# Up-projections of a two-layer trunk: all chunks 4 to 19 as pairs by seven products

## The chip, the cores and the metric

The kernel runs on one core of a Trainium2 chip. The metric is the device time of one execution in microseconds (us), the median of several runs. Five engines of the core work side by side, each through its own list of instructions in order: TensorE (PE, with its weight load PEld), VectorE (DVE), ScalarE (ACT), GpSimd (POOL) and SyncE (SP), which issues most of the transfers. An instruction that needs the result of another engine waits for it, and everything behind it on its own engine waits as well.

## What is computed

The reference is a decoder trunk of two layers over 512 tokens with 1024 channels in float32. A layer is an attention part and a feed-forward part, each with its norms and residual sums. The change concerns the first matrix product of the feed-forward part, whose inner size D_FF is 2816:

```python
def conv_ffn(xn, w_up, cw, cb, w_down):
    a = xn @ w_up                       # (512 x 1024) @ (1024 x 5632)
    ap = jnp.pad(a, ((0, 0), (CONV_W - 1, 0), (0, 0)))
    a = sum(ap[:, j:j + T] * cw[j] for j in range(CONV_W)) + cb
    gate, val = jnp.split(a, 2, axis=-1)
    return (jax.nn.gelu(gate, approximate=True) * val) @ w_down
```

## The kernel before

**Precision.** A float32 product is made of three passes of PE: each operand is split into a high part (a cast to `float32r`) and a low part (the operand less its high part), and `mm3` (L291) adds high x high (L292), high x low (L293) and low x high (L294). So each weight piece needs a cast on ACT and then its low half. The low half comes either from a DVE subtract, or in two steps: ACT writes the negated piece, rounded like the high part, to the place of the low part (a minus), and a transfer that POOL issues adds the unrounded piece to it in SBUF (an accumulating transfer, `accum_op=ALU.add`).

**Chunks.** The 2816 gate columns and 2816 value columns are taken in 22 chunks of 128 columns. A chunk has a gate half and a value half, each a PSUM bank of 128 columns by 512 tokens. A plain chunk loads two weight pieces of 1024 channels by 128 columns and does 8 channel blocks x 3 passes for each half, 48 matmuls over 512 tokens (`up`, L956).

**Seven products.** In the chunks listed in `SEVEN` (L28), 11 of the chunks 4 to 19, the product is written as a 2 x 2 block product: the weights in blocks by gate or value and by half of the channels (a11 and a12 for the gate, a21 and a22 for the value), the activations by half of the channels and half of the tokens (`LO`, `HI`). Seven products of sums replace eight: A11, S2, S3, A12, S1, A22 and S4, named by the weight block or sum of blocks in each, every one 4 channel blocks x 3 passes over 256 tokens (`half_mm`, L952), 84 matmuls in all. The sums of activations (`XA`, `XB`) are made once a layer (`sums_in`, L686). The sums of weights are made for each chunk by DVE (`weights_a`, L720, `weights_b`, L754). The sums of results are made on DVE in PSUM and in small tiles called `csum`, of which the first is an ACT copy of A11's result (L1000). In the program's order, the weights of a chunk are prepared one or two chunks ahead by generators whose steps the main loop (L978) advances between the products.

**Behind the product.** For each chunk, ACT writes the conv's last tap and bias to a tile `bb` (L655), DVE adds the two shifted taps for each half with two instructions (L656, L658), ACT applies GELU (L676), DVE multiplies gate and value (`product`, L673) and a transfer stores the result for the second matrix product (L671).

The instructions of each engine stand in the order in which the code emits them. Waits are derived from the tiles that an instruction reads and writes; a copy of one half of a PSUM bank and a product into the other half of it count as the same tile. The tiles come from rotating pools: `p8` (16 of 4 KB), `p4` (10) and `p2` (8), and 8 PSUM banks.

Of the kernel before, what the change touches and what calls it, by code (L numbers as in the profile page):

```python
# [27 lines left out]
SEVEN = 4, 5, 7, 8, 10, 11, 13, 14, 16, 17, 19  # L28

ADDED = (6, 9, 12, 15, 18), (18, 20)  # L30
# [87 lines left out]
def trunk_kernel(ctx, tc, x, norm_gains, w_qkv_a, w_o_a, w_q_b, w_o_b, kv_norm, w_kvf, b_f,  # L118
# [62 lines left out]
    def add_ffn(l):  # L181
        for c in range(NF):
            add_cols(w_up[l], c * 128)
            add_cols(w_up[l], DFF + c * 128)
# [461 lines left out]
    def ffn(l, bd, cp, nxt, ahead):  # L646
# [3 lines left out]

        def taps(c, banks, between=None):
            bb = t4([128, 2, T], name="bb")
            for s, ch in ((0, c), (1, NF + c)):
                ps = banks[s]
                act.activation(bb[:, s, :], ps, AF.Identity, bias=cp[:, 3, ch:ch + 1], scale=cp[:, 2, ch:ch + 1])  # L655
                dve.scalar_tensor_tensor(bb[:, s, 1:], ps[:, :T - 1], cp[:, 1, ch:ch + 1], bb[:, s, 1:],  # L656
                                         ALU.mult, ALU.add)
                dve.scalar_tensor_tensor(bb[:, s, 2:], ps[:, :T - 2], cp[:, 0, ch:ch + 1], bb[:, s, 2:],  # L658
                                         ALU.mult, ALU.add)
                if s == 0 and between is not None:  # L660
                    between()
            return bb
# [3 lines left out]
        def product():  # L666

            if gated:
# [4 lines left out]
                dve.tensor_tensor(hc[c], bb[:, 0, :], bb[:, 1, :], ALU.mult)  # L673
# [31 lines left out]
        halves, rest, late = {}, {}, []  # L705

        def split_pair(pair, src, n=1024):
            act.copy(pair[:, 0, :n], src)
            yield
            dve.tensor_tensor(pair[:, 1, :n], src, pair[:, 0, :n].bitcast(F32), ALU.subtract)  # L710

        def add_low(w, raw):

            act.activation(w[:, 1], raw, AF.Copy, scale=-1.0)
            pool.dma_start(w[:, 1], raw, accum_op=ALU.add)

        def sub_low(w, raw, n=1024):
            dve.tensor_tensor(w[:, 1, :n], raw, w[:, 0, :n].bitcast(F32), ALU.subtract)

        def weights_a(c):  # L720


            if c >= NF:
                return
            if c not in SEVEN:
                for i in range(2):
                    if c in ADDED[i]:
                        W.high_added()
                    else:
                        W.high()  # L730
                        W.low()
                    yield
                return
            r0, r1 = W.take(2)
            w = [t8([128, 2, 1024], F32R, name="w") for _ in range(2)]
            sa, sb = (t4([128, 1024], name="wsum") for _ in range(2))
            a11, a12, a21, a22 = r0[:, 0:512], r0[:, 512:1024], r1[:, 0:512], r1[:, 512:1024]
            act.copy(w[0][:, 0], r0)
            if c - 1 not in SEVEN:
                add_low(w[0], r0)  # L740
            dve.tensor_tensor(sa[:, 0:512], a11, a21, ALU.subtract)
            dve.tensor_tensor(sb[:, 0:512], a21, a22, ALU.add)
            yield
            dve.tensor_tensor(sa[:, 512:1024], sb[:, 0:512], a11, ALU.subtract)
            if c - 1 not in SEVEN:
                act.copy(w[1][:, 0], sa)
                add_low(w[1], sa)
            v = [t.rearrange("p s (q k c) -> p s q k c", q=2, k=4) for t in w]
            halves[c] = dict(A11=v[0][:, :, 0], A12=v[0][:, :, 1], S3=v[1][:, :, 0], S2=v[1][:, :, 1])
            rest[c] = w, r0, a12, a22, sa, sb  # L750

        def weights_b(c):

            if c not in rest:  # L754
                return
            (w0, w1), r0, a12, a22, sa, sb = rest.pop(c)
            if c - 1 in SEVEN:
                act.copy(w1[:, 0], sa)
                sub_low(w0, r0)
            w = [t8([128, 2, 1024], F32R, name="w") for _ in range(2)]  # L760
            dve.tensor_tensor(sb[:, 512:1024], a12, sa[:, 512:1024], ALU.subtract)
            act.copy(w[1][:, 0, 0:512], a22)
            if c - 1 in SEVEN:
                sub_low(w1, sa)
            yield
            act.copy(w[0][:, 0], sb)
            if c - 1 in SEVEN:
                late.append(lambda: sub_low(w[0], sb))
            elif c < SEVEN[-1]:
                add_low(w[0], sb)  # L770
            sub_low(w[1], a22, 512)
            if c == SEVEN[-1]:
                sub_low(w[0], sb)
            v = [t.rearrange("p s (q k c) -> p s q k c", q=2, k=4) for t in w]
            halves[c].update(S1=v[0][:, :, 0], S4=v[0][:, :, 1], A22=v[1][:, :, 0])
            yield

# [197 lines left out]
        steps = iter(())  # L975
        begun = None
        before = None
        for c in range(2, NF):  # L978
            if c == NF - 4:
                pair_load(0)  # L980
            steps = chain(steps, weights_b(c + 1), weights_a(c + 2))
            if c + 2 == SEVEN[0]:
                steps = chain(steps, weights_b(c + 2))
            if c in SEVEN:
                w = halves.pop(c)
                W.n_get += 2
                x11, x21, x22 = [(xT[0][i], xT[1][i], s) for i, s in ((0, LO), (1, LO), (1, HI))]
                if begun:
                    banks, s1, s17 = begun
                else:  # L990
                    banks = [bank([128, T], name="up") for _ in range(2)]
                    s1, s17 = (t2([128, 256], name="csum") for _ in range(2))
                s12 = t2([128, 256], name="csum")
                o1, o2, o3, o4 = banks[0][:, LO], banks[0][:, HI], banks[1][:, LO], banks[1][:, HI]

                def prod(o, a, x, start=False, w=w):
                    half_mm(o, w[a], x[0:2], x[2], start)

                def begin():
                    act.copy(s1, o1)  # L1000
                    prod(o3, "S3", (*XA, HI), True)
                    dve.tensor_tensor(s17, o3, s1, ALU.add)
                    prod(o2, "S2", (*XB, HI))

                def join():
                    dve.tensor_tensor(s12, o2, s1, ALU.add)

                if begun:
                    prod(o2, "S2", (*XB, HI))
                    product()  # L1010
# [899 lines left out]
```

## Time and profile before

| | us |
|---|---|
| time of one execution, median of 3 | 1096.97 (1096.6 to 1098.53) |
| span of the profiled execution | 1095.3 |
| PE busy in it | 1088.0 |
| DVE busy | 882.3 |
| ACT busy | 667.5 |
| POOL busy | 154.4 |

The profile is one execution. A row of a timeline has the start in us from the span's begin, the duration, the engine, the line of the code, the operation, what is written and read, and the shape; in brackets stands how long the engine had been idle and what released it. Neighbouring instructions of one kind can stand in one row with a count (x2). Durations of neighbours overlap by some 0.1 us, so the time an instruction occupies is read from the starts. A row of the grouped lines has the count, the total busy time, the mean duration in ns, and the idle time ahead with its releasers. A row of a window has its length, the busy time of PE, PEld, DVE, ACT and POOL with counts, the clock granted to PE as a share of full, the share of the transfer engines, and GB/s.

### The profile page before, as it was taken

What the parts mean: (1) busy time and instruction counts of PE and PEld (TensorE: products, weight loads), DVE (VectorE), ACT (ScalarE), POOL (GpSimd) and SP (SyncE); (2) the same over time, 40 slices, a digit from 0 to 9 for tenths busy, and PEclk for the clock granted to TensorE, in tenths of its full rate; (3) what the DMA queues carried; (4) which work ended last, traced back from release to release, by engine and by line L of the source; (5) the groups of instructions that cost most, each with busy time, mean ns of one, the idle gap of its engine ahead of it and who ended that gap; (6) DMA issues with size and microseconds to landing.
All of it is one profiled execution on the core that took longest, in us unless ns stands there. A gap on an engine that the chain in (4) does not pass through costs nothing.

```text
span 1095.3 us, 17965 instructions
## 1 busy us (share of the span) xinstructions
PE 1088.0 (99%) x6537; PEld 946.4 (86%) x6537; DVE 882.3 (81%) x1510; ACT 667.5 (61%) x1117; POOL 154.4 (14%) x240
## 2 busy tenths in 40 slices
PE   9999999999999999999999999999999999999997
PEld 7888889899999988888878888889899999988886
DVE  5898979877878789897686667858878788779895
ACT  6745665656666656576451587755755656647473
POOL 2643000111111111000001212100111111211000
PEclk9999999999999999999999999999999999999999
DMA  9899944668898979793447867784568978979872
GB/s 292 241 366 405 351 125 135 135 164 198 190 210 190 226 266 325 268 341 99 146 143 240 274 174 207 243 238 136 105 174 190 213 184 184 245 244 318 313 250 77
DMA packets 191984, 241.60 MB, mean 221 GB/s; under 512 B 12832, under 2 KB 139160, under 8 KB 191896
## 3 DMA queue, kind: packets, MB, share of 16 engines
q1 hardware_dynamic: 176552, 189.33, 53.6%
q0 software_dynamic: 14656, 51.13, 20.3%
q8 instruction: 51, 0.84, 0.3%
q14 instruction: 37, 0.30, 0.1%
q10 hardware_dynamic: 688, 0.01, 0.1%
HBM read 172.37 MB, written 39.73 MB: 194 GB/s over the span
## 4 chain that ended last, share of the span: by engine, by line
PE 95%; DMA 2%; issue 1%; DVE 1%; ACT 0%; SPq 0%; DVEq 0%; ACTq 0%; POOL 0%; POOLq 0%
PE up L294 12%; PE up L292 12%; PE up L293 12%; PE acc L292 9%; PE acc L294 9%; PE acc L293 9%; PE v_ps L293 2%; PE v_ps L292 2%; PE v_ps L294 2%; PE pT_ps L1751 2%; PE o_ps L1766 2%; PE s_ps L1717 2%; PE qk_ps L292 1%; PE first L292 1%; PE first L293 1%; PE first L294 1%
## 5 line engine op out<-in xcount | busy, mean ns | idle before, releaser
L292 PE MATMUL acc<-w 128*128 128x512 f32 (+1 forms) x311 | 120.5, 388 | 0.0
L294 PE MATMUL acc<-w 128*128 128x512 f32 (+1 forms) x311 | 120.4, 387 | 0.0
L293 PE MATMUL acc<-w 128*128 128x512 f32 (+1 forms) x267 | 103.2, 387 | 0.0
L292 PE MATMUL up<-xsh,w 128*128 128x256 f32 x352 | 99.6, 283 | 0.0
L293 PE MATMUL up<-xsl,w 128*128 128x256 f32 x352 | 99.6, 283 | 0.0
L294 PE MATMUL up<-xsh,w 128*128 128x256 f32 x352 | 99.6, 283 | 0.0
L655 ACT ACTIVATE bb<-up,conv 128x512 f32<-128x512 f32 x80 | 59.7, 776 | 59.2 <-DVE up L1046 48.4
L60 ACT CAST w<-wraw 128x1024 fp32r<-128x1024 f32 x81 | 83.2, 1051 | 18.6 <-DMA wraw<-in_w_up_dram 7.8
L294 PE MATMUL up<-xch,w 128*128 128x512 f32 (+1 forms) x276 | 93.5, 339 | 0.1
L292 PE MATMUL up<-xbh,w 128*128 128x512 f32 (+1 forms) x276 | 93.6, 339 | 0.0
L293 PE MATMUL up<-xcl,w 128*128 128x512 f32 (+1 forms) x276 | 93.5, 339 | 0.0
L293 PE MATMUL up<-xbl,w 128*128 128x512 f32 (+1 forms) x276 | 93.5, 339 | 0.0
L292 PE MATMUL up<-xch,w 128*128 128x512 f32 (+1 forms) x276 | 93.5, 339 | 0.0
L294 PE MATMUL up<-xbh,w 128*128 128x512 f32 (+1 forms) x276 | 93.4, 338 | 0.0
L78 DVE TENSOR_TENSOR w<-wraw,w 128x1024 fp32r<-128x1024 f32 x62 | 74.6, 1223 | 16.6 <-ACT w L60 16.2
L292 PEld LDWEIGHTS acc<-w 128*128 128x128 f32 x311 | 58.4, 188 | 11.9
L294 PEld LDWEIGHTS acc<-w 128*128 128x128 f32 x311 | 58.4, 188 | 11.8
L292 PEld LDWEIGHTS up<-xsh,w 128*128 128x128 f32 x352 | 67.6, 192 | 0.0
L293 PEld LDWEIGHTS up<-xsl,w 128*128 128x128 f32 x352 | 67.6, 192 | 0.0
L294 PEld LDWEIGHTS up<-xsh,w 128*128 128x128 f32 x352 | 67.6, 192 | 0.0
L656 DVE SCALAR_TENSOR_TENSOR bb<-up,conv,bb 128x511 f32<-128x511 f32 x80 | 59.5, 744 | 7.9 <-ACT bb L655 7.8
L98 POOL DMA_DIRECT2D w<-wraw x20 | 17.5, 876 | 336.8 <-ACT w L71 307.3
(317 smaller groups left out, 3112.8 us busy)
## 6 DMA issues: line engine op xcount, KB each, us to landing
wraw<-in_w_up_dram SPq DMA_DIRECT2D x88, 512.0 KB
w<-wraw POOLq DMA_DIRECT2D x32, 512.0 KB, 6.2
dT<-dsums SPq DMA_DIRECT2D x28, 512.0 KB
dsums<-in_w_down_dram SPq DMA_DIRECT2D x22, 512.0 KB
dsums<-in_w_down_dram SPq DMA_DIRECT2D x44, 256.0 KB
w<-wsum POOLq DMA_DIRECT2D x22, 512.0 KB, 5.6
hD<-hc POOLq DMA_DIRECT2D x44, 256.0 KB, 7.2
dact<-hD SPq DMA_DIRECT2D x44, 256.0 KB
```

The lines of the kernel that those rows point to most:

```text
L60: (copy or self.nc.scalar.copy)(pair[:, 0], raw)
L78: self.nc.vector.tensor_tensor(pair[:, 1], raw, pair[:, 0].bitcast(F32), ALU.subtract)
L98: self.nc.gpsimd.dma_start(pair[:, 1], raw, accum_op=ALU.add)
L292: pe.matmul(o, ah, bh, start=first, stop=False, skip_group_check=shared)
L293: pe.matmul(o, ah, bl, start=False, stop=False, skip_group_check=shared)
L294: pe.matmul(o, al, bh, start=False, stop=last, skip_group_check=shared)
L655: act.activation(bb[:, s, :], ps, AF.Identity, bias=cp[:, 3, ch:ch + 1], scale=cp[:, 2, ch:ch + 1])
L656: dve.scalar_tensor_tensor(bb[:, s, 1:], ps[:, :T - 1], cp[:, 1, ch:ch + 1], bb[:, s, 1:], ALU.mult, ALU.add)
L1717: pe.matmul(sc[j, i][hh][:, :nn], qT[j][own, qp, i * 128:(i + 1) * 128], k[own, kp, :nn], start=qp + kp == 0, stop=qp == 1)
L1751: pe.transpose(o[:, k0 + k, :], p[:, hh, k * 128:(k + 1) * 128], ident)
L1766: pe.matmul(o[64 * hh:64 * hh + 64, i * 128:(i + 1) * 128], Vt[hd // 8][:, k, (hd % 8) * 64:(hd % 8) * 64 + 64], pT[j, i, hh][:, k, :], st ...
```

## The change

`SEVEN` is replaced by `PAIRS`, pairs 2 to 9, so that chunks 4 to 19 all go by seven products, two chunks at a time. Chunks 2 and 3 ahead of them and 20 and 21 behind them stay plain.

- **Weight pieces.** A pair loads four pieces of half the channels by 256 columns: `ga` and `gb` of the gate, `va` and `vb` of the value. Each of the seven weight tiles of a pair is 1024 elements a partition and serves both chunks.
- **`prepare(p)`** (L728) makes the seven weight tiles in eight steps. `high` (L734) is a cast on ACT, `low` (L738) a subtract on DVE or POOL, and `added` (L741, L742) is the minus on ACT and the accumulating transfer. A12's low half and the sum `gb - ga` (L770) are on POOL; `ga - va` (L752), `va + vb` (L756) and `va - ga` (L758) on DVE. The low halves of S1, A22 and S4 come by accumulating transfers.
- **The gating product** (L686) is a POOL instruction.
- **Order of a pair on PE:** S2, S3, A12, S1, A22, then A11 of the next pair, then S4, each for both chunks. The steps of the next pair's preparation and the conv steps of the last pair's two chunks stand between them. All eight steps of the first pair's preparation stand in chunks 2 and 3, ahead of that pair's A11.
- **`keep_first`** (L1022) is the ACT copy of A11's results.

The core of the diff:

```diff
-SEVEN = 4, 5, 7, 8, 10, 11, 13, 14, 16, 17, 19
+PAIRS = range(2, 10)
...
+                for c0, k0 in ((0, 0), (DFF, 0), (DFF, 4), (0, 4)):
+                    add(lambda raw, c=c0 + c * 128, k0=k0: [(raw.rearrange("p (k c) -> p k c", k=4),
+                                                             cols(w_up[l], k0, 4, c, 256))])
...
-                dve.tensor_tensor(hc[c], bb[:, 0, :], bb[:, 1, :], ALU.mult)
+                pool.tensor_tensor(hc[c], bb[:, 0, :], bb[:, 1, :], ALU.mult)
...
+        def prepare(p):
+            def high(a, raw):
+                w[a] = t8([128, 2, 1024], F32R, name="w")
+                act.copy(w[a][:, 0], raw)
+                W2[p, a] = w[a].rearrange("p s (k c) -> p s k c", k=4)
+            def low(a, raw, engine=dve):
+                engine.tensor_tensor(w[a][:, 1], raw, w[a][:, 0].bitcast(F32), ALU.subtract)
+            def added(a, raw):
+                act.activation(w[a][:, 1], raw, AF.Copy, scale=-1.0)
+                pool.dma_start(w[a][:, 1], raw, accum_op=ALU.add)
+            w = {}
+            ga = grab(2)
+            high("A11", ga)
+            yield
+            low("A11", ga)
+            yield
+            va = grab(1)
+            s3 = t4([128, 1024], name="wsum")
+            dve.tensor_tensor(s3, ga, va, ALU.subtract)
+            high("S3", s3)
+            yield
+            vb = grab(1)
+            dve.tensor_tensor(va, va, vb, ALU.add)
+            yield
+            dve.tensor_tensor(ga, va, ga, ALU.subtract)
+            high("S2", ga)
+            gb = grab(1)
+            high("A12", gb)
+            yield
+            low("S2", ga)
+            low("A12", gb, pool)
+            high("S1", va)
+            added("S1", va)
+            yield
+            low("S3", s3)
+            pool.tensor_tensor(gb, gb, ga, ALU.subtract)
+            high("A22", vb)
+            added("A22", vb)
+            yield
+            high("S4", gb)
+            added("S4", gb)
+            yield
...
+        steps = prepare(PAIRS[0])
+        for c in (2, 3):
+            for s in range(2):
+                up(W.get(), banks[s], range(KD))
...
+                next(steps)
+                for _ in range(3):
+                    next(extra, None)
+                next(steps)
...
+        banks = begin(PAIRS[0])
+        s1 = keep_first(banks)
+        for p in PAIRS:
+            times(p, "S2", o2)
+            ends(pend)
+            for _ in steps:
+                pass
+            steps = nxt_steps
+            next(steps)
+            bbs = [biased(*pend[0][:2])]
+            next(steps)
+            times(p, "S3", o3, True)
+            sums(s12, o2, s1)
...
+            times(p, "A22", o3)
+            sums(o4, o2, s17)
+            next(steps)
...
+            if p + 1 in PAIRS:
+                later = begin(p + 1)
+            next(steps, None)
+            times(p, "S4", o2)
+            if p + 1 in PAIRS:
+                banks, s1 = later, keep_first(later)
```

Three places in the program's order show what moves, all where the first chunk by seven products begins in the first layer. The first is ACT, before the change. `w` tiles are weight tiles, `wsum` sums of weight blocks, `wraw` pieces as loaded, `bb` conv tiles, and `csum` the copy of A11's result:

```order
L766 CAST w_2272<-wsum_2230 128x1024
L714 ACTIVATE w_2272<-wsum_2230 128x1024
L655 ACTIVATE bb_2315<-up_2197,conv_1644 128x512
L655 ACTIVATE bb_2315<-up_2198,conv_1644 128x512
L738 CAST w_2326<-wraw_2223 128x1024
L676 ACTIVATE bb_2315<-bb_2315 128x512
L655 ACTIVATE bb_2379<-up_2286,conv_1644 128x512
L1000 COPY csum_2361<-up_2359 128x256
L655 ACTIVATE bb_2379<-up_2287,conv_1644 128x512
L758 CAST w_2327<-wsum_2328 128x1024
L762 CAST w_2452<-wraw_2225 128x512
```

The copy (L1000) stands behind two conv activations, a cast and a GELU, and ahead of the casts of the remaining weight tiles. The same place on ACT after the change:

```order
L734 CAST w_2310<-wraw_2138 128x1024
L734 CAST w_2314<-wraw_2270 128x1024
L689 ACTIVATE bb_2302<-bb_2302 128x512
L734 CAST w_2319<-wraw_2191 128x1024
L741 ACTIVATE w_2319<-wraw_2191 128x1024
L734 CAST w_2351<-wraw_2223 128x1024
L741 ACTIVATE w_2351<-wraw_2223 128x1024
L734 CAST w_2357<-wraw_2270 128x1024
L741 ACTIVATE w_2357<-wraw_2270 128x1024
L1022 COPY csum_2389<-up_2361 128x256
L1022 COPY csum_2389<-up_2363 128x256
L734 CAST w_2418<-wraw_2312 128x1024
```

The copies (L1022) stand behind the casts of S2, A12, S1, A22 and S4 in this order (the L734 rows) and three minus steps (L741). The cast of S4 reads `wraw_2270`, which is `gb`. On POOL, before the change, there are only issues of transfers at this place:

```order
L98 DMA w_2193<-wraw_2036 128x1024
L715 DMA w_2227<-wraw_2138 128x1024
L715 DMA w_2228<-wsum_2229 128x1024
L715 DMA w_2272<-wsum_2230 128x1024
L671 DMA hD_1936<-hc_2181 128x512
L671 DMA hD_1936<-hc_2313 128x512
L98 DMA w_2461<-wraw_2322 128x1024
```

After the change POOL has, besides those, two gating products, the low half of A12 and the sum `gb - ga` in the same queue:

```order
L96 DMA w_2193<-wraw_2036 128x1024
L684 DMA hD_1936<-hc_2181 128x512
L686 TENSOR_TENSOR hc_2300<-bb_2183 128x512
L738 TENSOR_TENSOR w_2314<-wraw_2270,w_2314 128x1024
L742 DMA w_2319<-wraw_2191 128x1024
L770 TENSOR_TENSOR wraw_2270<-wraw_2270,wraw_2138 128x1024
L742 DMA w_2351<-wraw_2223 128x1024
L742 DMA w_2357<-wraw_2270 128x1024
L684 DMA hD_1936<-hc_2300 128x512
L686 TENSOR_TENSOR hc_2451<-bb_2302 128x512
```

The sum (L770) writes `wraw_2270`, behind the low half of A12 (L738) and the issue of S1's accumulating transfer (L742). On PE, with what each instruction waits for, the last matmuls of A11 and the first of S2:

```order
L295 MATMUL up_2363<-xbh0_1815,w_2225 128x256
L296 MATMUL up_2363<-xbl0_1817,w_2225 128x256
L297 MATMUL up_2363<-xbh0_1815,w_2225 128x256
L295 MATMUL up_2361<-xsh_2264,w_2310 128x256 [waits Activation_49]
L296 MATMUL up_2361<-xsl_2265,w_2310 128x256 [waits DVE_49]
```

S2's first matmul (`w_2310`) writes the bank `up_2361` that the first `csum` copy reads, and waits for ACT.

More of the change, by code (lines that the diff above doesn't have):

```diff
@@ L752, in weights_b @@
[L752 to L764, printed above, removed]
-            yield
[L766 to L775, printed above, removed]
-            yield
+        W2 = {}
```

254 lines of the change are left out of this document (114 added, 140 removed).

## The prediction

> **What bounds the kernel now.** I read the page first, then the list of what TensorE (PE) waits for, then the timelines of the engines around the first chunk that goes by seven products, then the grouped lines for durations.
>
> ```profile
> PE 1088.0 (99%) x6537; PEld 946.4 (86%) x6537; DVE 882.3 (81%) x1510; ACT 667.5 (61%) x1117; POOL 154.4 (14%) x240
> PE warm L246 <- DVE zero L241: 1.2, 1, 1.2
> PE v_ps L293 <- DVE w L82: 0.2, 1, 0.2
> ```
>
> PE is busy for 1088.0 of 1095.3 us and its listed waits come to 1.4. So time is gained here only by giving PE less work, and a new wait of PE is paid in full. VectorE (DVE) is the next engine with 81%; GpSimd (POOL), with 14%, has room.
>
> **The gain: less work on PE.** A plain chunk is 48 matmuls of 512 columns, one by seven products 84 of 256. Their intervals stand in PE's timeline in the second layer (start, duration, engine, line):
>
> ```profile
> 887.81 0.39 PE L294 MATMUL up<-xch,w 128*128 128x512 f32 x1
> ...
> 889.85 0.39 PE L294 MATMUL up<-xch,w 128*128 128x512 f32 x1
> 904.83 0.28 PE L292 MATMUL up<-xsh,w 128*128 128x256 f32 x1
> ...
> 908.67 0.28 PE L294 MATMUL up<-xsh,w 128*128 128x256 f32 x1
> ```
>
> Nine steps of 512 columns take 2.04 us, 0.2267 each; 32 steps of 256 take 3.84, 0.120 each. A plain chunk is 48 x 0.2267 = 10.88 us, one by seven products 84 x 0.120 = 10.08: 0.80 less. Of chunks 4 to 19, 11 were by seven and now all 16 are: 5 more in each of two layers, 10 x 0.80 = 8.0 us. I add 0.5 for small hitches at the switches between the two kinds, which go too (an estimate): 8.5. With PE as busy as before the time is 1097.0 - 8.5 = 1088.5. The profiled span of 1095.3 is 1.7 under the median of 1097.0; I carry the difference over to the median.
>
> **The cost: a queue ahead of the first pair, once in each layer.** The second product of a pair, S2, adds into the banks that A11 has begun, and its first matmul waits for ACT's copy of A11's half bank (L1022). Before, that copy came early in ACT's order. Now the whole preparation of the first pair, eight steps, is emitted ahead of it. On ACT (ScalarE) the copy stands behind S4's cast and minus (L734, L741); the cast waits for POOL's `gb - ga` (L770); POOL reaches that behind A12's low half (L738) and the issue of S1's accumulating transfer (L742). I walk this queue on the clock of the trace in the first layer, with these rows:
>
> ```profile
> 198.55 0.75 DVE L658 SCALAR_TENSOR_TENSOR bb<-first,conv,bb 128x510 f32<-128x510 f32 x1
> 199.22 0.68 DVE L741 TENSOR_TENSOR wsum<-wraw 128x512 f32<-128x512 f32 x1
> 199.82 0.69 DVE L742 TENSOR_TENSOR wsum<-wraw 128x512 f32<-128x512 f32 x1
> ...
> 203.02 2.36 DVE L702 TENSOR_TENSOR xsl<-xsum,xsh 128x1024 fp32r<-128x1024 f32 x2
> ...
> 213.05 0.75 DVE L656 SCALAR_TENSOR_TENSOR bb<-up,conv,bb 128x511 f32<-128x511 f32 x1
> ...
> 215.94 0.68 DVE L741 TENSOR_TENSOR wsum<-wraw 128x512 f32<-128x512 f32 x1
> 201.95 1.99 ACT L701 CAST xsh<-xsum 128x1024 fp32r<-128x1024 f32 x2
> ...
> 220.15 0.37 ACT L1000 COPY csum<-up 128x256 f32<-128x256 f32 x1 [4.17 <-PE up L294]
> 218.51 0.28 PE L292 MATMUL up<-xbh,w 128*128 128x256 f32 x1
> L718 DVE TENSOR_TENSOR w<-wsum,w 128x1024 fp32r<-128x1024 f32 x22 | 26.8, 1218 | 1.0 <-ACT w L766 1.0
> L738 ACT CAST w<-wraw 128x1024 fp32r<-128x1024 f32 x22 | 22.8, 1036 | 0.0
> L676 ACT ACTIVATE bb<-bb 128x512 f32<-128x512 f32 x44 | 27.8, 632 | 14.7 <-DVE bb L658 14.6
> ```
>
> Occupancies: a 1024-column DVE step 2.36 - 1.22 = 1.14 us; a 512-column one 0.60 (199.22 to 199.82); the four conv steps of a chunk 2.89 (213.05 to 215.94); a 1024-column ACT step 1.99 - 1.04 = 0.95. Before, the copy ran at 220.15, while ACT had been idle for 4.17 us and A11 was just done.
>
> DVE is free of chunk 1's conv steps at 199.2, as before. Behind them stand, in the new order, two activation sums (1.26 and 1.2), two low halves of activations, A11's low half and `ga - va`: about 206.75. ACT casts S3 and two activation blocks, DVE follows with their low halves and `va + vb`: 212.25. Four conv steps, to 215.15; `ga = va - ga`, to 216.35. ACT: S2's cast to 217.35, A12's to 218.4, GELU (0.53), S1's cast and minus to 220.85, A22's to 222.75. POOL can start A12's low half at 218.4.
>
> What POOL takes for it, no row shows. The nearest ones are its rotary products, alone, and beside a DVE that combines two tiles of SBUF:
>
> ```profile
> 105.13 0.46 POOL L1142 TENSOR_TENSOR qk<-rope 128x128 f32<-128x128 f32 x1
> 105.55 0.47 POOL L1139 TENSOR_TENSOR rope<-qk,rope 128x128 f32<-128x128 f32 x1
> 105.97 0.32 POOL L1140 TENSOR_TENSOR rope<-qk,rope 128x64 f32<-128x64 f32 x1
> 106.25 0.32 POOL L1141 TENSOR_TENSOR rope<-qk,rope 128x64 f32<-128x64 f32 x1
> 73.51 0.91 POOL L1139 TENSOR_TENSOR rope<-qk,rope 128x128 f32<-128x128 f32 x1
> 74.38 0.77 POOL L1140 TENSOR_TENSOR rope<-qk,rope 128x64 f32<-128x64 f32 x1
> 75.11 0.77 POOL L1141 TENSOR_TENSOR rope<-qk,rope 128x64 f32<-128x64 f32 x1
> 66.35 0.69 DVE L625 TENSOR_TENSOR dsums<-dsums 128x512 f32<-128x512 f32 x1
> ...
> 73.15 3.28 DVE L625 TENSOR_TENSOR dsums<-dsums 128x512 f32<-128x512 f32 x4
> ```
>
> Alone, 64 more columns cost 0.42 - 0.28 = 0.14 us from start to start, 2.2 ns a column. I take 0.18 + 1024 x 2.2 ns = 2.4 us for a 1024-column step and 1.3 for a 512-column one. A lower bound is DVE's own 1.14; beside DVE the short ones grew by 0.45 each, and four DVE steps took 3.28 where 3 x 0.60 + 0.69 = 2.49 was due, so each engine waits for the other. [...]
>
> POOL then: A12's low half until 220.8 alone; but S3's low half (1.14) runs on DVE at 218.5, and turn-taking makes it 221.9. The issue of S1's transfer occupies about 0.6 (rows below), `gb - ga` 2.4 more: 223.8 to 224.9. ACT's S4 cast and minus take 1.9 and the first copy 0.3. S2 starts at 226.1 to 227.1. A11's 24 matmuls end at 218.51 + 24 x 0.12 = 221.39. So PE waits 4.7 to 5.7 us; if POOL's gating product of chunk 1 also delays DVE near 200, 0.9 more, 6.6. With both POOL steps at DVE's 1.14, the floor, it would be 4.7 - 2.5 = 2.2. I take 5.7, nearest the contested rows. The second layer has the same rows 578.32 to 578.33 us later, so this comes twice:
>
> ```profile
> 781.35 2.36 DVE L702 TENSOR_TENSOR xsl<-xsum,xsh 128x1024 fp32r<-128x1024 f32 x2
> 798.47 0.37 ACT L1000 COPY csum<-up 128x256 f32<-128x256 f32 x1 [4.17 <-PE up L294]
> ```
>
> **The clock behind that wait.** What a cold PE costs shows at the start, and when it goes cold at the end:
>
> ```profile
> 5.53 0.63 PE L1361 MATMUL qk_ps<-w,xal 128*128 128x512 f32 x1
> ...
> 7.46 0.40 PE L1361 MATMUL qk_ps<-w,xah 128*128 128x512 f32 x1
> 1088.00:1090.00 2.00, 1.53 (x12) 1.25 (x10) 1.71 (x4) 1.07 (x4) 0.00 (x0) 1.00 0.43 161
> 1090.00:1095.00 5.00, 0.00 (x0) 0.00 (x0) 2.04 (x5) 0.39 (x3) 0.00 (x0) 0.69 0.41 145
> ```
>
> A 512-column matmul takes 0.63 early and 0.40 from 7.46 on; PE begins at 1.2, behind the wait listed first, and the change lies between these two rows, so some 5 us ran slowly; at half speed 2.4 us of that was lost (an estimate). At the end PE stops near 1089.5; a granted clock of 0.69 over 1090 to 1095 is 38% at full and 62% at half, so it fell about 1.9 us into that window, 2.4 us after the last matmul. A wait of 5.7 us is beyond that. I take 2.4 us lost each time; the ends are 0 (the wait falls short of it) and 2.6. [...]
>
> **The steady pairs.** A pair has 20.16 us of PE. DVE has in it six 1024-column steps, eight conv steps and ten sums out of PSUM:
>
> ```profile
> L1046 DVE TENSOR_TENSOR up<-up,csum 128x256 f32<-128x256 f32 x22 | 9.5, 433 | 32.5 <-PE up L294 32.5
> 904.67 0.42 DVE L1006 TENSOR_TENSOR csum<-up,csum 128x256 f32<-128x256 f32 x1 [0.42 <-PE up L294]
> 905.01 0.74 DVE L656 SCALAR_TENSOR_TENSOR bb<-up,conv,bb 128x511 f32<-128x511 f32 x1
> L715 POOL DMA_DIRECT2D w<-wsum x22 | 18.8, 854 | 90.4 <-ACT w L714 53.1 <-DVE up L1046 23.3 <-DVE wsum L742 10.6
> 213.18 1.43 POOL L671 DMA_DIRECT2D hD<-hc  x2
> L655 ACT ACTIVATE bb<-up,conv 128x512 f32<-128x512 f32 x80 | 59.7, 776 | 59.2 <-DVE up L1046 48.4 <-PE up L294 10.8
> ```
>
> 6 x 1.14 + 2 x 2.89 + 10 x 0.34 = 16.0 us (0.34 from 904.67 to 905.01). ACT: ten 1024-column steps, four conv activations and two GELUs at their 0.78 and 0.63 less 0.1 of overlap, two copies: 9.5 + 2.7 + 1.1 + 0.5 = 13.8. POOL: 2 x 2.4 + 2 x 1.3 + five issues at 1.43 - 0.85 = 0.58 make 10.3. None reaches 20.16 alone. If every POOL step blocks DVE wholly, DVE comes to 16.0 + 7.4 = 23.4, above it. The conv steps take their input from PSUM and can run beside POOL's, so I expect some 2.7 of the 7.4 to bite: 18.7. There is a longer loop from one pair's `ga` to the next pair's: `ga`, S2 and A12 casts, A12's low half, S1's issue, `gb - ga`, S4's cast and minus, A11's cast and low half, two pairs of sums, `ga - va`, four conv steps, `va + vb`. By engine that is DVE 4 x 1.14 + 4 x 0.34 + 2.89, ACT 5 x 0.95, POOL 2 x 2.4 + 0.6: 19.0 us without turn-taking and some 22 with 2.7 of it. It stands at the edge, and what the wait at the start leaves prepared is used up before PE feels it: I take 0.6 us a layer, ends 0 and 5. The gating product costs DVE 0.6 less a chunk and is not waited for by PE: nothing, hidden in POOL's free 10 us. Weight pieces of 256 columns have 1 KB runs instead of 512 B and the same bytes: nothing, while PE waits for no transfer, and below nothing at the hitches counted above.
>
> **Sum.** -8.5 + 2 x (5.7 + 2.4 + 0.6) = +8.9: 1097.0 + 8.9 = 1105.9, so 1106.
>
> **Rivals.** *The queue is done in time* (faster): if POOL's steps and the casts ended 5 us sooner, S2 would follow A11 at once, and the time would be 1088.5. For it speaks that ACT was idle for 4.17 us ahead of its copy; against it, that the new ACT order fills this with casts bound to POOL. It decides at 221.4 on the first layer's clock. *A short wait, clock kept* (about the same): POOL nearer to DVE's pace, a wait of 2.2 to 3.5 and hardly a fall of the clock: 1088.5 + 2 x 2.2 = 1092.9 to 1088.5 + 2 x (3.5 + 1) = 1097.5; it decides at about 1.7 us for a 1024-column step of POOL. Against it stand the rows at 2.2 ns a column. *The turn-taking saturates the steady pairs* (slower): at 22 us a loop, 1.8 over PE's 20.16, from about the fifth of eight pairs on, 4 or 5 times, 5 us a layer beyond the sum: 1116; with DVE's 23.4 in each pair, 1125. That the change doesn't convert its chunks is excluded by PE's order.
>
> **How the numbers follow.** Forecast 0.62, time 1106 with 1100 to 1111 as its own bounds (a wait of 4.7 with 1.5 of clock and no drift below; 6.6, 2.6 and 2 of drift above). In time: 0.10. Short wait: 0.12, of which 0.02 faster and 0.10 the same. Saturated: 0.16. A measurement of this kernel can tell about 0.2%, 2.2 us, from no change. Faster 0.12, the same 0.10, slower 0.78. The range leaves out the queue that is done in time and the far end of saturation: 1096 to 1118.
>
> **What would show it.** Right: PE idle of 5 to 6 us twice, at S2's first matmul, released by ACT's copy; behind it 256-column matmuls at about twice 0.28 us and a granted clock below 1; POOL's 1024-column steps at 2.4 us or more; 256-column intervals of 0.12 in 16 chunks a layer. Wrong: no wait there (then the order of the queue does not bind), or waits spread over the pairs (then it is the turn-taking), or 1024-column POOL steps near 1.2.

## The result, and the profile after

| | before | after |
|---|---|---|
| time of one execution, median | 1097.62 (4 runs) | 1106.7 (4 runs, 1105.87 to 1109.06) |
| ratio to before, 95% interval | | 1.0087 (1.0072 to 1.0101) |
| span of the profiled execution | 1095.3 | 1104.1 |

The change is 0.9% slower, near the forecast of 1106. Every ratio here is to the kernel before as it was timed beside that run; its medians lie between 1096.9 and 1097.6. One of the 11 executions of the kernel before with the gating product on GpSimd, described below, took 6144.57 us in the slow state, and its ratio goes by the other ten. First the engines on the page and the list of what PE waits for (total, times, longest):

```profile
PE 1083.4 (98%) x6897; PEld 960.3 (87%) x6897; DVE 900.8 (82%) x1462; ACT 683.8 (62%) x1133; POOL 306.8 (28%) x318
PE up L295 <- ACT csum L1022: 12.5, 2, 6.3
PE acc L297 <- DVE w L821: 1.3, 2, 0.7
PE warm L249 <- DVE zero L244: 1.2, 1, 1.2
```

PE is busy 4.6 us less and yet the span is 8.8 longer. Two waits, one in each layer, for ACT's copy hold nearly all of it. PE's timeline at the first, and the windows around it (PE busy, PEld, DVE, ACT, POOL, granted clock):

```profile
220.68 0.28 PE L297 MATMUL up<-xbh,w 128*128 128x256 f32 x1
227.27 0.58 PE L295 MATMUL up<-xsh,w 128*128 128x256 f32 x1 [6.31 <-ACT csum L1022]
...
230.43 0.41 PE L297 MATMUL up<-xsh,w 128*128 128x256 f32 x1
...
230.84 0.28 PE L296 MATMUL up<-xsl,w 128*128 128x256 f32 x1
222.00:224.00 2.00, 0.00 (x0) 0.00 (x0) 0.58 (x1) 1.25 (x2) 2.00 (x2) 0.99 0.51 98
224.00:226.00 2.00, 0.00 (x0) 0.00 (x0) 0.00 (x0) 1.04 (x2) 1.77 (x2) 0.50 0.88 164
```

S2 was due at 220.80 and starts at 227.27: 6.47 us. The clock falls at about 224, 3 us after A11's last matmul, and the first 16 matmuls of S2 take 3.57 us (227.27 to 230.84) in place of 1.92: 1.65 lost. In the second layer the same two are 6.30 and 1.94; the expectations below have 2.06 for the second, which counts one matmul too few. The queue behind it, on POOL, ACT and DVE:

```profile
201.22 1.60 POOL L686 TENSOR_TENSOR hc<-bb 128x512 f32<-128x512 f32 x1
219.01 2.49 POOL L738 TENSOR_TENSOR w<-wraw,w 128x1024 fp32r<-128x1024 f32 x1 [16.19 <-ACT w L734]
221.66 0.89 POOL L742 DMA_DIRECT2D w<-wraw  x1 [0.16 <-issue]
222.28 2.64 POOL L770 TENSOR_TENSOR wraw<-wraw 128x1024 f32<-128x1024 f32 x1
222.20 1.05 ACT L741 ACTIVATE w<-wraw 128x1024 fp32r<-128x1024 f32 x1
224.96 1.04 ACT L734 CAST w<-wraw 128x1024 fp32r<-128x1024 f32 x1 [1.70 <-POOL wraw L770]
225.91 1.05 ACT L741 ACTIVATE w<-wraw 128x1024 fp32r<-128x1024 f32 x1
226.87 0.62 ACT L1022 COPY csum<-up 128x256 f32<-128x256 f32 x2
201.49 3.57 DVE L715 TENSOR_TENSOR xsl<-xsum,xsh 128x1024 fp32r<-128x1024 f32 x2 [0.38 <-ACT xsh L714]
219.17 3.42 DVE L738 TENSOR_TENSOR w<-wsum,w 128x1024 fp32r<-128x1024 f32 x1
```

The order is the one that was walked: A12's low half, S1's issue, `gb - ga`, then on ACT S4's cast, its minus and the copies. Of the two engines it is DVE that lost most: S3's low half took 3.42 us for 1.22, until POOL's 2.49 us step was over.

In the later pairs PE waits for nothing, and one pair takes 20.16 us. The sum of the differences: a pair's 20.16 against 20.69 on the average before (165.55 us for chunks 4 to 19 of the first layer) is -4.27 a layer, and -0.3 for a hitch near 909 in the second layer of the kernel before; 6.47 + 6.30 for the waits, 1.65 + 1.94 for the clock, 1.9 for the stops at L821 (PE waits 0.67 us in each layer and falls 0.95 behind by its starts); and -0.6 that the two traces differ by in their first 35 us, ahead of the feed-forward part. That is +8.8, as the spans show.

### The profile page after: what moved, and what is told of

It is laid out like the page before. It is cut to its first block, busy times and chain, and to the rows that moved or that the text cites. A ratio compares the mean times of both kernels' runs of the same rounds, so it can differ in the third digit from the quotient of the medians.

```text
span 1104.1 us, 18905 instructions
## 1 busy us (share of the span) xinstructions
PE 1083.4 (98%) x6897; PEld 960.3 (87%) x6897; DVE 900.8 (82%) x1462; ACT 683.8 (62%) x1133; POOL 306.8 (28%) x318
## 4 chain that ended last, share of the span: by engine, by line
PE 88%; issue 5%; DVE 3%; ACT 2%; DMA 1%; POOL 1%; SPq 0%; DVEq 0%; POOLq 0%; ACTq 0%
PE up L295 9%; PE up L296 9%; PE up L297 9%; PE acc L297 9%; PE acc L295 8%; PE acc L296 8%; PE v_ps L295 2%; PE v_ps L296 2%; PE v_ps L297 2%; PE qk_ps L1396 2%; PE pT_ps L1786 2%; PE o_ps L1801 2%; PE s_ps L1752 2%; DVE w L821 1%; PE first L297 1%
## 5 line engine op out<-in xcount | busy, mean ns | idle before, releaser
L295 PE MATMUL up<-xsh,w 128*128 128x256 f32 x512 | 146.9, 287 | 12.5 <-ACT csum L1022 12.5
L296 PE MATMUL up<-xsl,w 128*128 128x256 f32 x512 | 146.4, 286 | 0.0
L297 PE MATMUL up<-xsh,w 128*128 128x256 f32 x512 | 146.3, 286 | 0.0
L734 ACT CAST w<-wraw 128x1024 fp32r<-128x1024 f32 x96 | 97.2, 1043 | 76.8 <-DVE wraw L758 59.1
L686 POOL TENSOR_TENSOR hc<-bb 128x512 f32<-128x512 f32 x44 | 76.7, 1743 | 226.6 <-ACT bb L689 143.2
L664 DVE SCALAR_TENSOR_TENSOR bb<-up,conv,bb 128x511 f32<-128x511 f32 (+1 forms) x160 | 118.7, 745 | 6.0 <-ACT bb L670 3.2
L295 PEld LDWEIGHTS up<-xsh,w 128*128 128x128 f32 x512 | 100.0, 195 | 12.9 <-ACT csum L1022 12.9
L297 PEld LDWEIGHTS up<-xsh,w 128*128 128x128 f32 x512 | 99.8, 195 | 0.0
L296 PE MATMUL up<-xbl,w 128*128 128x256 f32 (+1 forms) x256 | 79.3, 310 | 0.0
L296 PE MATMUL up<-xcl,w 128*128 128x256 f32 (+1 forms) x256 | 79.3, 310 | 0.0
L295 PE MATMUL up<-xbh,w 128*128 128x256 f32 (+1 forms) x256 | 79.3, 310 | 0.0
L295 PE MATMUL up<-xch,w 128*128 128x256 f32 (+1 forms) x256 | 79.2, 310 | 0.0
L297 PE MATMUL up<-xch,w 128*128 128x256 f32 (+1 forms) x256 | 79.2, 310 | 0.0
L297 PE MATMUL up<-xbh,w 128*128 128x256 f32 (+1 forms) x256 | 79.2, 309 | 0.0
L58 ACT CAST w<-wraw 128x1024 fp32r<-128x1024 f32 x61 | 62.3, 1057 | 17.5 <-PE v_ps L296 6.9
```

The source lines that it names most:

```text
L58: (copy or self.nc.scalar.copy)(pair[:, 0], raw)
L295: pe.matmul(o, ah, bh, start=first, stop=False, skip_group_check=shared)
L296: pe.matmul(o, ah, bl, start=False, stop=False, skip_group_check=shared)
L297: pe.matmul(o, al, bh, start=False, stop=last, skip_group_check=shared)
L664: dve.scalar_tensor_tensor(bb[:, s, n:], ps[:, :T - n], cp[:, 2 - n, ch:ch + 1], bb[:, s, n:], ALU.mult, ALU.add)
L686: pool.tensor_tensor(hc[c], bb[:, 0, :], bb[:, 1, :], ALU.mult)
```

## The experiments

**Where the wait comes from.** The queue theory says that the copy's place in ACT's order makes the wait. The first two runs move it for the first pair alone, ahead of A22's step and ahead of S4's step:

```diff
+                    if c == 3:
+                        first = begin(PAIRS[0])
+                        begun = first, keep_first(first)
                     next(steps)          # the step with A22; the other run: one step later
...
-        banks = begin(PAIRS[0])
-        s1 = keep_first(banks)
+        banks, s1 = begun
```

> Edit: in the changed kernel the first pair's A11 and its ACT copy are emitted ahead of the first pair's preparation steps for A22 and S4, so that on ACT the copy stands behind S1's minus (which ended at 221.36 in the first layer) and no longer behind S4's cast. Queue theory (ours): the copy runs at about 221.3, S2 starts at about 221.7, the waits of 6.3 us at S2 shrink to about 0.9 us in each layer, the clock stays full, so the 1.65 and 2.06 us lost to it go as well: 1106.7 - 5.5 - 5.4 - 3.7 = 1092, faster than before by about 5. Rival A (the time is lost in the steady pairs, where DVE and GpSimd take turns): the pairs have no spare time, what was prepared ahead is missing now and PE waits inside the pairs: not under 1100. Rival B (S2 needs GpSimd's results themselves, not the copy): wait stays 6 us, 1106.

> Edit: as the run with the copy ahead of A22, but the copy is emitted one step later, ahead of S4's step alone: on ACT behind A22's minus (ended at 223.25), not behind S4's cast, which waits for GpSimd. Queue theory: the copy runs at 223.2, S2 at about 223.5, a wait of 2.7 us in each layer in place of 6.3. The granted clock of the changed kernel fell about 3 us after A11's last matmul, so it should stay full: 1106.7 - 3.7 - 3.6 - 3.7 = 1095.7; if it falls nevertheless, up to 1099.5. Rival A (steady pairs): not under 1100. Rival B (S2 needs GpSimd's results): 1106.

Measured: 1102.47, ratio 1.005 (1.0031 to 1.0069), and 1105.71, 1.0078 (1.0063 to 1.0093). The waits at S2 did what the theory says: 0.87 and 0.68 us in the first run, 2.76 and 2.56 in the second. The time did not: 4 us and 1 us were gained where 15 and 11 were expected. The clock, which was to stay full, fell to 0.50 in both runs; in the second, S2 and S3 together took 1.4 and 1.6 us longer than at the full clock. In the first run PE met this instead, at A12 (PE, then DVE and ACT):

```profile
222.80 0.39 PE L295 MATMUL up<-xsh,w 128*128 128x256 f32 x1 [0.71 <-ACT csum L1004]
...
230.74 0.39 PE L295 MATMUL up<-xbh,w 128*128 128x256 f32 x1 [1.93 <-DVE csum L1049]
229.13 1.23 DVE L738 TENSOR_TENSOR w<-wraw,w 128x1024 fp32r<-128x1024 f32 x1 [5.40 <-ACT w L734]
230.27 0.75 DVE L1049 TENSOR_TENSOR csum<-up,csum 128x256 f32<-128x256 f32 x2
226.15 1.05 ACT L734 CAST w<-wraw 128x1024 fp32r<-128x1024 f32 x1 [1.22 <-POOL wraw L770]
227.11 1.05 ACT L741 ACTIVATE w<-wraw 128x1024 fp32r<-128x1024 f32 x1
228.06 1.03 ACT L734 CAST w<-wraw 128x1024 fp32r<-128x1024 f32 x1
```

A12 waits for the sums s12, which stand in DVE's order behind A11's low half of the next pair; that waits for an ACT cast behind S4's cast, which waits for GpSimd. The queue reached PE by a second way. The clock fell again, 0.5 us after PE had resumed: the granted clock is 0.81 over 230 to 232 and 0.50 over 232 to 234. In the second run the second layer showed something else: from its second pair on PE waited in each pair, soon 0.9 us each and 21.15 us apart. The four executions of the first run lie at 1100.5, 1100.9, 1104.1 and 1104.2; only the second of these was traced, and what the slower two did is not known.

**GpSimd's steps back on DVE.** One run moves A12's low half and `gb - ga`, the other the gating product:

```diff
-            low("A12", gb, pool)
+            low("A12", gb)
-            pool.tensor_tensor(gb, gb, ga, ALU.subtract)
+            dve.tensor_tensor(gb, gb, ga, ALU.subtract)
```
```diff
-                pool.tensor_tensor(hc[c], bb[:, 0, :], bb[:, 1, :], ALU.mult)
+                dve.tensor_tensor(hc[c], bb[:, 0, :], bb[:, 1, :], ALU.mult)
```

> Edit: in the changed kernel A12's low half and gb - ga run on DVE in place of GpSimd, in all pairs; the gating product stays on GpSimd and ACT's order stays. Queue theory: GpSimd's pace is only a part of the wait. DVE makes the two at 219.2 and 221.5 to 222.6, S4's cast then waits for A22's minus (223.2), the copy runs at 225.1, S2 at 225.5: the wait shrinks by 1.8 us in each layer, to about 4.6, and the clock still falls: 1106.7 - 3.6 = 1103, within 1101 to 1104. Steady pairs: DVE gains 2.3 us of work a pair and loses fewer blocked spells, no wait of PE either way. Rival (GpSimd's two long steps and the turn-taking are the whole cause): the waits go and the time falls to 1090.

> Edit: the gating product goes back to DVE, all else as changed. Queue theory: near 201 the product on GpSimd held two DVE low halves for 1.2 us (3.57 for two in place of 2.36), while on DVE it costs 0.6: the wait at S2 shrinks by about 0.6 in each layer. The waits of 0.65 us at the start of the second product (L821), which the kernel before has not, go if GpSimd's product at 399.5 causes them: 1106.7 - 1.2 - 1.3 = 1104.2. In the steady pairs DVE gets 1.2 us more work and is blocked less: nothing. Rival (the product on GpSimd costs nothing anywhere): 1106.7; rival (DVE is nearly full in the pairs): slower than 1107.

Measured: 1118.82, ratio 1.0195 (1.018 to 1.021), and 1129.22, 1.0288 (1.0273 to 1.0304). Both expectations of the total failed (a rival of the second, that DVE is nearly full in the pairs and the time above 1107, had the outcome right), while the wait at S2 came out as walked in the first (4.66 and 4.45 us) and nearly in the second (6.11 and 5.87). What was missed are the later pairs. One pair of each as a window, of the changed kernel, with the sums on DVE, and with the product on DVE:

```profile
300.16:320.32 20.16, 20.16 (x170) 20.16 (x169) 17.19 (x25) 14.19 (x18) 12.09 (x10) 1.00 0.84 211
```
```profile
298.20:320.10 21.90, 20.41 (x168) 20.21 (x168) 20.09 (x27) 14.15 (x18) 7.25 (x7) 1.00 0.78 193
```
```profile
319.76:341.87 22.11, 20.66 (x169) 20.25 (x169) 17.94 (x27) 14.15 (x19) 9.52 (x7) 1.00 0.77 191
```

A pair takes 21.90 and 22.11 us. With the sums on DVE, DVE is busy for 20.09 of 21.90. With the product there it is busy for 17.94 only, so no engine is full; it is the loop from one pair's `ga` to the next pair's that is too long. Two rows of that run (DVE, then POOL) show it:

```profile
318.14 1.23 DVE L738 TENSOR_TENSOR w<-wraw,w 128x1024 fp32r<-128x1024 f32 x1 [3.94 <-ACT w L734]
```
```profile
330.55 3.35 POOL L738 TENSOR_TENSOR w<-wraw,w 128x1024 fp32r<-128x1024 f32 x1 [9.04 <-DVE up L1044]
```

DVE idles for 3.94 us behind ACT's cast, which is in the queue behind GpSimd's steps, and one of these takes 3.35 us. PE's first wait in the pairs comes only in the third or fourth of them: until then it lives on what the wait at S2 let the other engines prepare. With the product on DVE the waits for L821 grew as well, to 2.5 us in each layer by PE's starts, where the expectation had them go if the product on GpSimd was their cause.

**A second theory.** So in the changed kernel the loop stands close to PE's 20.16, and the theory is that the wait at S2 is also a head start: the preparation runs during it, and the later pairs live on what it leaves. Remove the wait and PE meets the loop. The next run takes the second way of the queue out as well, the one after it shortens the first pair's own queue:

```diff
-            next(steps)                  # A11's low half of the next pair
             times(p, "S3", o3, True)
             sums(s12, o2, s1)
+            next(steps)
```
```diff
-                low("A12", gb, pool)     # gb - ga in the same way
+                low("A12", gb, dve if p == PAIRS[0] else pool)
```

> Edit: as the run with the copy ahead of A22, and in every pair DVE's sums s12 (A11 + S2) stand ahead of the low half of the next pair's A11 instead of behind it. In that run A12 waited 2.09 us in each layer for s12, which stood in DVE's order behind that low half, which waited for an ACT cast behind S4's cast, that is for GpSimd's gb - ga: the same queue reached PE by a second way, and the clock fell again (some 1.7 us lost). Theory (each queued wait is one place in the order): the second wait and the second fall of the clock go, 1102.5 - 2 x 3.8 = 1095, a little under the kernel before. Rival (the pairs' loop over DVE, ACT and GpSimd is full, so that PE only meets the same lag at a later product): a new wait of 1 to 2 us stands at A11, S4 or S3 of the next pair, and the time stays at 1099 to 1103.

> Edit: as the run with copy and s12 moved, and in the first pair alone A12's low half and gb - ga run on DVE, which is idle there for 5 us, in place of GpSimd. In the other pairs they stay on GpSimd. Theory: S4's cast of the first pair comes about 2 us earlier, so whatever lag was left behind the first pair shrinks by about 2 us a layer: 1091 to 1094. Rival (the loop of the later pairs is full by itself): no faster than the run without this edit, with waits in the later pairs.

Measured: 1103.4, ratio 1.0053 (1.0036 to 1.007), and 1103.01, 1.0052 (1.0037 to 1.0067). The rivals held both times, though the first of them had put longer waits, of 1 to 2 us, at other products. The clock stays full (0.998 to 1.0 granted on the average of each execution) and A12 no longer waits, but PE waits at S2 in 13 pairs, 8.5 us in all (first of the two runs), 21.15 us apart:

```profile
PE up L295 <- ACT csum L1004: 8.5, 13, 1.2
327.66 0.39 PE L295 MATMUL up<-xsh,w 128*128 128x256 f32 x1 [0.74 <-ACT csum L1004]
348.81 0.39 PE L295 MATMUL up<-xsh,w 128*128 128x256 f32 x1 [0.73 <-ACT csum L1004]
344.12 1.22 DVE L738 TENSOR_TENSOR w<-wraw,w 128x1024 fp32r<-128x1024 f32 x1
344.26 3.38 POOL L738 TENSOR_TENSOR w<-wraw,w 128x1024 fp32r<-128x1024 f32 x1 [1.00 <-ACT w L734]
```

The same two instructions in the changed kernel, in a pair at the same place:

```profile
322.40 2.41 POOL L738 TENSOR_TENSOR w<-wraw,w 128x1024 fp32r<-128x1024 f32 x1 [1.00 <-ACT w L734]
324.15 0.43 DVE L1044 TENSOR_TENSOR up<-up,csum 128x256 f32<-128x256 f32 x1 [1.01 <-PE up L297]
324.50 1.40 DVE L738 TENSOR_TENSOR w<-wraw,w 128x1024 fp32r<-128x1024 f32 x1
```

In the changed kernel DVE still waits for PE's results at 324.15, so GpSimd's step begins first and takes 2.41. With the wait removed DVE is there first, by 0.14 us, and GpSimd's step takes 3.38. That 0.97 us is the difference between a loop that fits and 21.15. For this step who comes first decides it, and a late PE puts GpSimd first.

The run with the copy ahead of S4 shows both cases in one execution, the first layer and then the second:

```profile
320.12 2.41 POOL L738 TENSOR_TENSOR w<-wraw,w 128x1024 fp32r<-128x1024 f32 x1 [1.01 <-ACT w L734]
340.33 2.42 POOL L738 TENSOR_TENSOR w<-wraw,w 128x1024 fp32r<-128x1024 f32 x1 [1.00 <-ACT w L734]
903.59 3.36 POOL L738 TENSOR_TENSOR w<-wraw,w 128x1024 fp32r<-128x1024 f32 x1 [1.01 <-ACT w L734]
924.74 3.36 POOL L738 TENSOR_TENSOR w<-wraw,w 128x1024 fp32r<-128x1024 f32 x1 [1.01 <-ACT w L734]
```

With the short step the pairs follow each other after 20.21 us, with the long one after 21.15. In the changed kernel the step is short in all pairs of both layers, and from the third pair on comes every 20.2 us, the last one of the second layer excepted. That is only 0.05 over PE's 20.16, so little of the head start is used up there: the wait helps mainly by putting GpSimd first. How late PE must be stays open: waits of 2.76 us at S2 in the first layer of this run were enough and 2.56 in its second were not, while 0.68 at S2 and 2.09 at A12 were enough in the run with the copy ahead of A22, but for the last pair of its second layer.

**The clock by itself.** 46 matmuls of 256 columns stand in the changed kernel's wait:

```diff
         banks = begin(PAIRS[0])
+        for i in range(46):
+            pe.matmul(spare[:, LO], wa[:, 0, i % 4, 0:128], xT[0][0][:, i % 4, LO], start=True, stop=True)
         s1 = keep_first(banks)
```

> Edit: in the changed kernel 46 matmuls of 256 columns, whose result nobody reads, stand on PE between A11 and S2 of the first pair, in each layer, in a bank that is already read. They take 5.5 us of the wait of 6.3. If the half clock behind the wait is due to PE's idle time, it goes, and the 1.65 and 2.06 us with it: 1106.7 - 3.7 = 1103. The wait for the copy itself ends at the same moment as before. Rival (the slow matmuls behind the wait have another cause, such as transfers or late weights): 1106.7, with the slow matmuls still there.

Measured: 1104.09, ratio 1.0062 (1.0047 to 1.0077), 2.6 us under the changed kernel; the stretch from the first 256-column matmul of a layer to the second product is 1.46 and 1.78 us shorter. The slow matmuls are gone, the granted clock is 1.00 all the way from 218 to 232, and S2 starts no earlier than before:

```profile
228.17 0.39 PE L295 MATMUL up<-xsh,w 128*128 128x256 f32 x1 [0.87 <-ACT csum L1024]
228.39 0.28 PE L296 MATMUL up<-xsl,w 128*128 128x256 f32 x1
```

So PE's idleness is the cause of the fall, which costs some 3 us of the 9.

**The loop shortened.** If A12's low half alone goes to DVE, `gb - ga` starts earlier and DVE has less to do than with both. The next run does this on top of the moved copy and s12; another one also puts the gating products of the layer's last four chunks on DVE; a third takes the kernel before and moves the product to GpSimd:

```diff
-            low("A12", gb, pool)
+            low("A12", gb)
```
```diff
-                pool.tensor_tensor(hc[c], bb[:, 0, :], bb[:, 1, :], ALU.mult)
+                (dve if c >= 2 * PAIRS[-1] else pool).tensor_tensor(hc[c], bb[:, 0, :], bb[:, 1, :], ALU.mult)
```

> Edit: as the run with copy and s12 moved, and A12's low half runs on DVE in all pairs; gb - ga and the gating product stay on GpSimd. In that run each pair took 21.15 us, 1.0 over PE's 20.16, and A12's low half took 3.36 us on GpSimd (2.41 in the changed kernel), as it began just behind a DVE subtract. Theory (the loop through both engines is the bound, and a wait of one for the other in it is what makes 20.2 into 21.15): on DVE the step costs 1.14, gb - ga starts 2 us earlier, the loop is near 19, and PE's waits at S2 in the later pairs (8.5 us in all with the first) shrink to the 0.9 and 0.7 of the first pair. Time 1103.4 - 7 = 1096, within 1093 to 1098. Rival (DVE's own list is the bound, as where both steps were on it, 21.9 us a pair): 21 us a pair or more, not under 1103.

> Edit: as the run with A12's low half on DVE, and the gating products of chunks 18 to 21, the last ones of a layer, run on DVE. Theory (GpSimd's product at the layer's end delays DVE's low halves L821, for which PE waits 1.1 to 1.2 us in each layer at the start of the second product): these waits go, some 2 us less than the run without this edit. Rival (DVE is as late with the products in its own list): no difference, or PE waits at L821 as long as before.

> Edit: the kernel before, with the gating product on GpSimd; nothing else of the change. Theory (the product on GpSimd is hidden while the loop has room, and costs PE only where DVE's next steps are awaited): PE has no waits in the kernel before, DVE loses 0.6 us of work a chunk and gains blocked spells, so PE's waits stay near none in the chunks, and 0.65 us come at L833 or its like at the start of the second product in each layer, as in the changed kernel: 1097.2 + 1.3 = 1098.5, within 1097 to 1100. Rival (moving the product to GpSimd is itself the larger cost of the change): 1102 or more; rival (it is a gain): under 1096.

Measured: 1096.25, ratio 0.9991 (0.9982 to 1.0); 1097.39, 0.9999 (0.999 to 1.0008); 1097.14, 0.9997 (0.9988 to 1.0006). The first is 7 us under the run without it, as the loop theory said; its rival, that DVE's own list is the bound, asked for 1103 or more. The product on GpSimd costs the kernel before nothing, and no wait for the low halves of the second product appears there, so that expectation of 1.3 us failed. The wait for L821 does not go with the products on DVE either (0.75 us). In the changed kernel the product does delay those low halves (DVE and POOL):

```profile
408.34 3.59 DVE L821 TENSOR_TENSOR w<-wraw,w 128x1024 fp32r<-128x1024 f32 x2
408.40 1.31 POOL L686 TENSOR_TENSOR hc<-bb 128x512 f32<-128x512 f32 x1
```

but it is not the only thing that does; the rest of the order at a layer's end was not taken apart.

**The version that beats both.** In the run with A12's low half on DVE, S2 of the second pair still waited 1.39 us for copies behind A22's minus. The last two runs move all copies up to A11, and then the first A11 ahead of chunk 3's second half:

```diff
                 later = begin(p + 1)
+                later = later, keep_first(later)
...
-                banks, s1 = later, keep_first(later)
+                banks, s1 = later
```
```diff
                     bb = taps(*before)
+                    first = begin(PAIRS[0])
+                    begun = first, keep_first(first)
                     next(steps)
```

> Edit: as the run with A12's low half on DVE, and in the later pairs, too, ACT's copies of A11's results stand right behind A11, ahead of the step with A22's cast and minus. In the run without this edit S2 of the second pair waited 1.39 us in each layer for these copies, which stood on ACT behind A22's minus, with A11 done 2.9 us earlier. Theory: those waits go and nothing takes their place, as ACT reaches the copies after A11 has ended: 1096.25 - 2.8 - about 0.5 of smaller ones = 1093, within 1092 to 1095. Rival (ACT now waits for A11 and brings A22 and S4 late, or the lag only moves on): 1096.

> Edit: as the run with the later copies moved, and the first pair's A11 stands on PE ahead of the second half of chunk 3, and its copies on ACT right behind the conv activations of chunk 2. A11's weights were ready some 10 us earlier and ACT was idle there for 5 us. Theory: the first pair's waits of 0.87 and 0.68 us at S2 go as well, 1.5 less than the run without this edit: 1091.5, within 1090 to 1094; against the kernel before 0.995. What would be left of the ideal 1088.5 are the waits of 0.67 us for L821 in each layer. Rival (S2 then waits for its own low half on DVE, or the copies hold up the casts of S2 and A12): no difference.

Measured: 1093.29, ratio 0.9964 (0.9951 to 0.9976), and 1093.49, 0.9965 (0.9953 to 0.9978). The waits of 1.39 went and nothing took their place. The last step gained nothing: the first pair's 0.87 and 0.68 at S2 became 1.03 and 1.75 at A22, behind DVE's sums. What PE waits for in the first of these:

```profile
PE acc L297 <- DVE w L821: 1.3, 2, 0.7
PE up L295 <- ACT csum L1004: 1.3, 2, 0.7
PE up L295 <- DVE csum L1049: 0.8, 1, 0.8
```

Seven products for all chunks are worth 3.6 us, once ACT's and DVE's orders and one step of GpSimd's are changed.

## Why the prediction was right, step by step

- **The gain**: 8.5 was forecast, 2 x 4.27 + 0.3 = 8.8 came.
- **The queue**: place, releaser and order were right in both layers. The wait was 6.47 and 6.30, not 5.7. POOL's steps took 2.49 and 2.64 (2.4 forecast). The term that was too small is DVE's delay by the product on GpSimd near 201, which had been left at the range's end (6.6): two low halves took 3.57 us, 1.2 more than before, and everything behind them came late. Against that, GpSimd began A12's low half just ahead of DVE's subtract (219.01 against 219.17), so it did not pay the 1.1 us of turn-taking that the forecast gave it; DVE paid. So the 1.2 us show only in part: the wait is 0.77 and 0.60 over the forecast's 5.7.
- **The clock**: it fell, but 1.65 and 1.94 us were lost and not 2.4. The step that failed is the reading of the start: 5 us at half speed. In the trace before, the granted clock is listed as 1.00 over those first microseconds, and as 0.50 only from 1091.9 on. Here the slow stretch is 3.4 and 4.1 us, and a slow 256-column matmul takes 0.213 us, 1.8 times its 0.120. The run with the filled wait shows that the idle time is the cause.
- **The steady pairs**: 0.6 a layer was forecast and none came. The sum of the loop, 19.0 and 22 with turn-taking, was a good one: 20.2 here, 21.15 with one collision more. That conv steps run beside POOL's the changed kernel shows: two took 1.52 us at 305.59 (0.75 for one in the kernel before), within POOL's `gb - ga` of 2.79 us that began at 305.15. But the loop and the wait were taken as separate terms. The runs show that they are one: the wait is what keeps PE clear of the loop, and without it PE's listed waits in the later pairs come to some 7 us.
- **The layer's end** was judged free; PE waits 0.67 us for L821 in each layer and loses 0.95 by its starts. The run with the last products on DVE shows that the product alone isn't the cause.
- **The rivals**: "the queue is done in time" was priced at 1088.5. The runs that took the first wait nearly away gave 1102.5 and 1103.4, so the price was wrong as long as the loop is what it is, and the third rival, the saturated loop, is what stands behind the first term. GpSimd as such was not the cost: taking its steps back cost 12 and 22 us more. Two sums of the third rival don't follow from its rows: 4 or 5 times 1.8 us is 7 to 9 us a layer, of which the sum holds 0.6, and not the 5 beyond the sum that give 1116; and 23.4 in each of 16 pairs is 52 us over PE's 20.16, far more than 1125 allows.

That the total came so near is partly luck: 0.8 and 0.6 more for the waits, 0.7 and 0.5 less for the clock and 0.3 less by the larger gain, in each layer 0.6 less for the pairs and 0.95 more at the end, and 0.6 less in the first 35 us, which has nothing to do with the change.

## What to carry to other kernels

When a program prepares work ahead of PE, follow each engine's order from the first instruction that PE waits for back through every queue, and look for a small instruction, such as a copy, that stands behind work it doesn't need. Before a wait is priced as pure loss, ask what the other engines do during it: a loop through them that is as long as PE's own work is hidden by that wait, and shows as soon as it is removed. Such a loop can be the bound though no engine in it is full: with the product on DVE a pair took 22.11 us with DVE busy for 17.94.

## What the runs showed of the hardware

- Where a DVE and a GpSimd instruction that each combine two operands in SBUF overlapped in time, one delayed the other; in most rows it was the later one that was delayed: GpSimd's 1024-column step took 2.41 us ahead of DVE's subtract (322.40 in the changed kernel) and 3.38 when it began 0.14 behind it (344.26 in the run with the copy ahead of A22 and s12 moved), and DVE's subtract took 3.42 for 1.22 when it began 0.16 behind GpSimd's step (219.17 in the changed kernel). Not in all rows: at 228.47 there, DVE's subtract began 0.15 ahead of GpSimd's product, and took 2.85 to the product's 1.61. DVE's sums out of PSUM took 0.43 us beside GpSimd's step of 2.41 (322.71 and 324.15), as in the kernel before.
- In the feed-forward part the granted clock fell to 0.50, 3.2 and 3.7 us after PE's last matmul in the changed kernel and 2.3 and 3.4 us after it in the run with the copy ahead of S4; in the run with the copy ahead of A22 it fell 2.6 and 2.9 us after it, when PE had been back at work for 0.5 to 0.8 us. A wait of 1.86 us by PE's starts (the run with the sums on DVE, near 908) left it at 1.00; one of 2.09 (at A12 above) did not.
